# Attention products over 64 features with all 128 rows of TensorE in both passes

## The chip, the core and the metric

The kernel runs on one core of a Trainium2 chip: TensorE (the matrix engine, 128 rows by 128 columns), VectorE, ScalarE, GpSimd, the on-chip memory SBUF, the accumulators of TensorE in eight banks of PSUM, and DMA queues to HBM. The metric is the device time of one execution in microseconds, the median of several runs. TensorE's clock has two levels, 1.2 and 2.4 GHz; the profile gives the granted share of the higher one.

## What is computed

One encoder layer over 512 tokens of 1024 features: a SwiGLU FFN, a projection, sparse attention beside a gated convolution, an output projection, a second FFN and a gated embedding, each of the first parts with a layer norm. The attention chooses 128 keys for each query by an indexer and runs a softmax over these. All values are float32.

```python
x = layer_norm(A * x + 0.5 * swiglu(x, ffn1...))
q, k, v, qi, ki, wi, bg, cg, u = split(x @ w_in)      # 8 heads x 64; ki: 64; wi: 8
score = sum_h relu(qi[h] @ ki.T) * wi[h]              # chunk-causal keys only
idx = top_k(score, 128)
attn[h] = softmax(q[h] @ k[h][idx].T / 8 - slope[h] * |dist|) @ v[h][idx]
conv = bg * causal_conv3(cg * u)
x = layer_norm(A * x + concat(attn, conv) @ w_out)
x = layer_norm(A * x + 0.5 * swiglu(x, ffn2...))
out = x + sigmoid(x @ ple_gate_w) * (p @ ple_proj_w)
```

## The kernel before

Every float32 operand is split into a high part, rounded to the type that TensorE multiplies in one pass (`F32R`), and a low part, the rest. `split` (L110 to L112) does it: a ScalarE cast (L111), then a VectorE subtraction (L112). `mm` (L127 to L133) makes a product from three passes over such parts, high by high, high by low, low by high, one matmul each at L132, which is the line of nearly all matmuls.

Tokens are handled in four blocks of 128. The order of the work is: first FFN; the first block of values v; the indexer's keys `ki` and queries `qi`; the scores (L541 to L555: for query blocks 1 to 3, eight heads each, one product at L506 and L507, a ScalarE relu at L550, a VectorE accumulation at L552 or L554); the choice of keys (`choose`, L563 and L566, 16 rounds on VectorE) interleaved with TensorE's projections of v, the convolution and queries and keys (`qk_proj`), 24 matmuls each; attention; the output projection; the second FFN; the gate. A scheduler places the instructions of each engine in the order of the program, changed by priorities: weights are loaded and split ahead of their use by a number of instructions (`unit`, L114 to L122). Each engine then runs its own list in order.

A product over a head's 64 features does not use `mm`. `stack` (L492) puts the high parts of a head's queries on 64 of the 128 rows and the low parts on the other 64. `mm64` (L504 to L507) then takes two passes: both halves of the rows by the keys' high parts, which stand there twice (L506, 128 rows), and the high half alone by the keys' low parts (L507, 64 rows). The indexer's keys `ki` have high and low parts on both halves already. In `qk_proj` (L610) the high parts of a pair of heads' keys go to `kT[j]`, copied to the other half by ScalarE at L622; the low parts of two pairs share one page, `kL[j // 2]`, and stand on one half only. 24 such products belong to the scores, 32 to the logits.

In attention, `softmax(h)` (L665) makes four products of query block t by (t + 1) x 128 keys, and for each a VectorE pass from the bank (L676), an exponential on ScalarE (L677), a reciprocal and a multiplication on VectorE (L678, L679). `av(h)` (L681) transposes the ten 128 x 128 blocks of probabilities on TensorE (L693), splits them (three banks), pulls one item of filling work, and multiplies by v: for each of the four key blocks three passes of `mm` at L703 with the pair's 128 columns of v as weights, of which the head's 64 are used, into the one bank of the group "av". The split at L708 writes the head's half of `attnT[j]`. `softmax(h + 1)` is issued ahead of `av(h)`; two items of filling work (the last pair's projection, the convolution's rows of the output projection, the embedding's projection) come with each head. The pages of v hold all high parts, then all low parts.

Pages of 4 KiB a partition are taken from a list of 38, the one free for longest first.

Of the kernel before, what the change touches and what calls it, by code (L numbers as in the profile page):

```python
# [12 lines left out]
P = 128  # L13
# [15 lines left out]
# places on chip, and how far ahead of its use (in instructions) each kind of weights is asked for  # L29
# [34 lines left out]
def layer_kernel(ctx: ExitStack, tc: tile.TileContext, x, ln1_g, ln1_b, ffn1_wg, ffn1_wu, ffn1_wd, w_in,  # L64
# [17 lines left out]
    # 4 KiB pages, the one that has been free for longest first  # L82
# [31 lines left out]
    def unit(src, shape, ahead=AHEAD):  # L114
        """1024 weights a partition, loaded and split: pages of high and low parts."""
        with tc.high_priority(offset=ahead):
            r = page(shape, F32)
            nc.sync.dma_start(r, src)
            hi, lo = page(shape), page(shape)
            split(hi, lo, r)  # L120
            free(r)
        return hi, lo  # L122
# [4 lines left out]
    def mm(ps, pairs, first=True, last=True):  # L127
        """sum over pairs of (stationary (high, low), moving (high, low))"""
        n = len(pairs)
        for i, (st, mv) in enumerate(pairs):  # L130
            for k, (a, b) in enumerate(PASSES):
                nc.tensor.matmul(ps, lhsT=st[a], rhs=mv[b], start=first and i == 0 and k == 0,  # L132
                                 stop=last and i == n - 1 and k == 2)  # L133

    # ---- tokens on partitions (nat) and features on partitions (xT, high and low parts)
# [31 lines left out]
    def both(tile2, *idx):  # L167
        """(high, low) of a page [P, 2, n]"""
        return tuple(tile2[(slice(None), k) + idx] for k in range(2))

    # Operands of the seven products, by quarters: features' halves and tokens' halves
    class Quarters:
        """x, features on partitions: quarters (feature half, token half) and the sums of them"""
# [6 lines left out]
        def slot(self, name):  # L180
            """high and low parts' places"""
            if name in ("B11", "B21", "B22", "T1"):
                i = ("B11", "B21", "B22", "T1").index(name)
                self.q[name] = [self.big[k][:, i] for k in range(2)]
            else:
                self.q[name] = [page([P, 4, 256]) for k in range(2)]
                if name != "B12":
                    self.pages += self.q[name]
            return self.q[name]

        def block(self, t, group):
            """tokens' block t; returns the copies to be made of it"""
# [15 lines left out]
        def load(self, src, h, n):  # L208
            """a quarter from DRAM, features on rows there"""
            self.raw[h, n] = page([P, 4, 256], F32)  # L210
            nc.sync.dma_start(self.raw[h, n], rows(src[:, n * 256:(n + 1) * 256], h * 512, 4))
# [4 lines left out]
        def copies(self, todo):  # L216
            for r, p3, lo in todo:
                # one reader of a bank at a time
                cp = nc.scalar.copy(r, p3)
                tc.add_manual_dep(getattr(cp, "ins", cp), getattr(lo, "ins", lo).name,  # L220
                                  mybir.DependencyInfo(mybir.DependencyClass.Sync, mybir.DependencyReason.DATA), reason="bank")
# [17 lines left out]
    def ffn(X, wg, wu, wd, ln_g, ln_b, first, load_nat, groups, nplain, ahead, ahead_f, ahead_d):  # L239
        """nat <- LN(nat + 0.5 / alpha * swiglu(x)); returns its transpose."""  # L240
# [10 lines left out]
        def plain(fc, ws, cuts, ah):  # L251
            """one chunk of hidden features, each product computed"""
# [16 lines left out]
        def weights(w, fc, ops, pages):  # L269
            """the seven products' weights for two chunks, step by step: (high, low), [P, 4, P] each"""  # L270
# [31 lines left out]
        def two(fc, ah):  # L302
            """two chunks of hidden features by seven products"""
# [8 lines left out]
            def prod(a, b):  # L312
                """a product for gate and up"""
# [5 lines left out]
            # e: chunk by chunk, token halves of gate and up; k: partial sums  # L319
# [85 lines left out]
    # the per-layer embedding's input, features on partitions, and its weights  # L405
# [10 lines left out]
    def embed(t):  # L416
        """the per-layer embedding's projection"""
# [9 lines left out]
    # ---------------------------------------------------------------- start  # L427
# [3 lines left out]
    with tc.high_priority(offset=10000), tc.manual_schedule():  # L431
# [8 lines left out]
        # until x is there, the tensor engine warms up  # L440
# [18 lines left out]
    # ---------------------------------------------------------------- projections  # L459
    def colT(u, group, tok0=0, m=P):  # L460
        """columns' projection, features on partitions"""
        ps = bank(group)
        mm(ps[:m, :S - tok0], [((u[0][:, c], u[1][:, c]), (x1T[0][:, c, tok0:], x1T[1][:, c, tok0:])) for c in range(NDC)])
        free(*u)
        return ps[:, :S - tok0]
# [4 lines left out]
    # v, tokens on partitions  # L470
# [3 lines left out]
    def v_proj(blocks):  # L474
        for t in blocks:
            ps = bank("main")
            mm(ps, [((x1T[0][:, c, ts(t)], x1T[1][:, c, ts(t)]), (wv[c // 2][0][:, c % 2], wv[c // 2][1][:, c % 2])) for c in range(NDC)])
            v.append(page([P, 2, 512]))
            split(v[t][:, 0], v[t][:, 1], ps)
# [8 lines left out]
    # A product over a head's 64 features takes two passes: high and low parts of the queries, one above  # L488
    # the other, by the keys' high parts twice; then the queries' high parts by the keys' low parts.
    HALF = (slice(0, 64), slice(64, 128))  # L490

    def stack(dst, ps, scale=None):  # L492
        """two heads' queries: high parts where the head is, low parts in the other half"""
# [10 lines left out]
    def mm64(ps, q, e, at, k_hi, k_lo):  # L504
        """a head's queries by its keys"""
        nc.tensor.matmul(ps, lhsT=q[:, e, at], rhs=k_hi, start=True, stop=False)  # L506
        nc.tensor.matmul(ps, lhsT=q[HALF[e], e, at], rhs=k_lo[HALF[e]], start=False, stop=True)  # L507

    # indexer keys and weights, then queries
# [20 lines left out]
    # minus the distance, and minus BIG where a key isn't admissible or not among the chosen  # L530
# [10 lines left out]
    # scores and the choice of keys: query block 0 chooses every admissible key  # L541
# [33 lines left out]
    # short convolution  # L575
# [27 lines left out]
    # queries are scaled by 1 / (8 slope), exactly  # L603
# [6 lines left out]
    def qk_proj(j, group):  # L610
# [5 lines left out]
        kT[j] = page([P, 2, 512])  # L616
        if j % 2 == 0:
            kL[j // 2] = page([P, 2, 512])
        for e in range(2):
            here, there = HALF[e], HALF[1 - e]  # L620
            split(kT[j][here, e], kL[j // 2][here, j % 2], ps[here])
            nc.scalar.copy(kT[j][there, e], kT[j][here, e].bitcast(F32))  # L622
# [4 lines left out]
    def out_conv():  # L627
        """the convolution's rows of the output projection"""
# [32 lines left out]
    # attention, a head at a time  # L661
# [3 lines left out]
    def softmax(h):  # L665
        """exp(logits - max) / sum, queries on partitions"""
# [4 lines left out]
        for t in range(NTB):  # L671
# [3 lines left out]
            mm64(ps[:, :w_], qT[j], e, ts(t), kT[j][:, e, :w_], kL[j // 2][:, j % 2, :w_])  # L675
# [5 lines left out]
    def av(h, fill):  # L681
        j, e = h // 2, h % 2
        a = soft[h]
        # keys on partitions: blocks 0, then 1 and 3, then 2
# [17 lines left out]
        for b in range(NTB):  # L702
            mm(po[:, b * P:], [(both(v[b], slice(j * P, (j + 1) * P)), pT[b])], first=b == 0, last=b == NTB - 1)  # L703
# [3 lines left out]
        pr = slice(e * 64, (e + 1) * 64)  # L707
        split(attnT[j][pr, 0], attnT[j][pr, 1], po[pr])  # L708
# [5 lines left out]
    for h in range(NH):  # L714
# [4 lines left out]
        if h % 2:  # L719
            free(qT[h // 2], kT[h // 2])  # L720
        if h % 4 == 3:
            free(kL[h // 4])
# [3 lines left out]
    # output projection, attention's rows  # L726
# [23 lines left out]
    # ---------------------------------------------------------------- second FFN  # L750
    x3T = ffn(X, ffn2_wg, ffn2_wu, ffn2_wd, ln3_g, ln3_b, {}, None, GROUPS2, NPLAIN2, AHEAD2, AHEAD_F2, AHEAD_D2)

    # ---------------------------------------------------------------- per-layer embedding
# [41 lines left out]
```

## Time and profile before

| | us |
|---|---|
| median of 3 runs (1041.1 to 1044.16) | 1044.11 |
| span of the profiled execution | 1039.8 |
| TensorE matmuls busy | 1026.4 |
| VectorE busy | 819.2 |
| ScalarE busy | 432.7 |

The profiled execution is one run; its span goes from the first to the last instruction. A matmul's recorded duration holds its way through the array, so neighbours overlap; the distance between the starts of two matmuls tells what one takes of a full engine. Weight loads have rows of their own (PEld) and may lie under the matmul before. Line numbers are those of the kernel before.

### The profile page before, as it was taken

The numbers are of one execution on the slowest core, as the hardware profiler recorded it, in microseconds if no ns is written. First come the engines' busy times: TensorE is split into PE (matmuls) and PEld (weight loads), VectorE is DVE, ScalarE is ACT, GpSimd is POOL, SyncE is SP. The second block draws the span as 40 slices with busy tenths as digits, with TensorE's granted clock in tenths as the row PEclk, the third lists the DMA queues.
The fourth block names the chain that finished last, engine by engine and source line by source line (L and its number), as shares of the span: only waits on it lengthen the run. The fifth ranks groups of instructions, "written<-read, shape, count | busy, mean of one in ns | idle before, by whom it ended". The sixth has DMA issues, their size and how long they took to land.

```text
span 1039.8 us, 15540 instructions
## 1 busy us (share of the span) xinstructions
PE 1026.4 (99%) x6345; PEld 909.6 (87%) x6345; DVE 819.2 (79%) x1275; ACT 432.7 (42%) x605; POOL 24.9 (2%) x35
## 2 busy tenths in 40 slices
PE   8999999999999999999999999999999999999998
PEld 7989899898998785888877778989999899998887
DVE  7997868878798947999467889986877968688852
ACT  6444434334344335332565636442524434245221
POOL 1000000000001200000000001000000000000100
PEclk9999999999999999999999999999999999999999
DMA  9432324323236220422111323331424313227111
GB/s 315 134 119 82 105 79 143 101 82 122 82 132 184 61 81 21 132 72 74 48 61 61 102 61 102 99 103 44 162 82 140 103 59 105 83 83 255 50 49 51
DMA packets 99511, 104.59 MB, mean 101 GB/s; under 512 B 5872, under 2 KB 81904, under 8 KB 99440
## 3 DMA queue, kind: packets, MB, share of 16 engines
q1 hardware_dynamic: 99440, 103.60, 31.6%
q8 instruction: 50, 0.82, 0.3%
q14 instruction: 21, 0.17, 0.1%
HBM read 101.49 MB, written 2.10 MB: 100 GB/s over the span
## 4 chain that ended last, share of the span: by engine, by line
PE 93%; DMA 3%; DVE 2%; ACT 1%; issue 0%; POOL 0%; POOLq 0%; SPq 0%; DVEq 0%; ACTq 0%
PE bk L132 88%; PE bk L507 2%; PE bk L506 1%; ACT pg L111 1%; DMA pg<-in_w_in_dram 1%; PE bk L693 1%; DMA pg<-in_ffn_wu_dram 1%; DVE pg L112 1%; DMA pg<-in_x_t_dram 1%; DMA pg<-in_ffn_wd_dram 1%; PE bk L146 1%; DVE nat L162 0%; PE bk L201 0%; POOL mv L160 0%; DVE st L738 0%
## 5 line engine op out<-in xcount | busy, mean ns | idle before, releaser
L132 PE MATMUL bk<-pg,pg 128*128 128x256 f32 (+2 forms) x2928 | 512.3, 333 | 3.0 <-ACT pg L111 2.6
L132 PEld LDWEIGHTS bk<-pg,pg 128*128 128x128 f32 x2928 | 442.4, 190 | 58.5 <-ACT pg L111 4.7
L111 ACT CAST pg<-pg 128x1024 fp32r<-128x1024 f32 (+1 forms) x267 | 260.1, 985 | 312.5 <-PE bk L132 78.3
L112 DVE TENSOR_TENSOR pg<-pg,pg 128x1024 fp32r<-128x1024 f32 (+1 forms) x267 | 301.1, 1140 | 39.5 <-ACT pg L111 31.0
L132 PE MATMUL bk<-xq,pg 128*128 128x256 f32 x2208 | 274.2, 284 | 1.6 <-DVE pg L112 0.8
L132 PEld LDWEIGHTS bk<-xq,pg 128*128 128x128 f32 x2208 | 269.3, 192 | 4.5 <-ACT pg L111 1.8
L132 PE MATMUL bk<-xT,pg 128*128 128x512 f32 (+2 forms) x600 | 133.6, 382 | 0.3 <-ACT xT L111 0.2
L132 PEld LDWEIGHTS bk<-xT,pg 128*128 128x128 f32 (+1 forms) x600 | 109.8, 186 | 22.3 <-issue 0.6
L132 PE MATMUL bk<-pg,xT 128*128 128x512 f32 (+1 forms) x312 | 71.6, 381 | 1.4 <-DVE nat L385 1.4
L132 PEld LDWEIGHTS bk<-pg,xT 128*128 128x128 f32 x312 | 54.4, 188 | 14.6 <-issue 2.8
L329 ACT ACTIVATE a<-pg 128x512 f32<-128x512 f32 x40 | 25.2, 629 | 69.5 <-DVE pg L338 63.3
L111 ACT CAST pg<-hf 128x512 fp32r<-128x512 f32 x48 | 29.7, 618 | 37.0 <-DVE hf L330 19.7
L399 DVE SCALAR_TENSOR_TENSOR nat<-bk,nat 128x512 f32<-128x512 f32 x64 | 40.4, 684 | 0.8 <-PE bk L132 0.7
L112 DVE TENSOR_TENSOR pg<-bk,pg 128x512 fp32r<-128x512 f32 (+2 forms) x45 | 27.6, 637 | 14.5 <-ACT pg L111 14.2
L338 DVE TENSOR_TENSOR pg<-bk,pg 128x512 f32<-128x512 f32 x20 | 13.8, 692 | 31.7 <-PE bk L132 31.4
L111 ACT CAST pg<-bk 128x512 fp32r<-128x512 f32 (+2 forms) x45 | 23.0, 548 | 36.6 <-PE bk L132 33.4
L330 DVE TENSOR_TENSOR hf<-a,pg 128x512 f32<-128x512 f32 x40 | 27.6, 689 | 12.6 <-ACT a L329 12.6
L112 DVE TENSOR_TENSOR pg<-hf,pg 128x512 fp32r<-128x512 f32 x48 | 32.9, 686 | 4.2 <-ACT pg L111 4.2
L160 POOL TENSOR_TENSOR mv<-mv,mhalf 128x1 f32<-128x1 f32 x12 | 17.8, 1479 | 644.3 <-DVE mv L159 644.3
L286 DVE TENSOR_TENSOR pg<-pg,pg 128x512 f32<-128x512 f32 x40 | 27.3, 687 | 5.9 <-DMA pg<-in_ffn_wg_dram 5.9
L292 DVE TENSOR_TENSOR pg<-pg 128x512 f32<-128x512 f32 x40 | 27.5, 688 | 2.8 <-PE bk L132 2.8
L287 DVE TENSOR_TENSOR pg<-pg,pg 128x512 f32<-128x512 f32 x40 | 27.4, 687 | 0.0
(96 smaller groups left out, 589.7 us busy)
## 6 DMA issues: line engine op xcount, KB each, us to landing
pg<-in_ffn_wg_dram SPq DMA_DIRECT2D x44, 512.0 KB, 3.8
pg<-in_ffn_wu_dram SPq DMA_DIRECT2D x44, 512.0 KB, 4.7
pg<-in_ffn_wd_dram SPq DMA_DIRECT2D x44, 512.0 KB, 4.0
pg<-in_w_in_dram SPq DMA_DIRECT2D x28, 512.0 KB, 3.6
pg<-in_w_out_dram SPq DMA_DIRECT2D x8, 512.0 KB, 3.5
pg<-in_ple_gate_w_dram SPq DMA_DIRECT2D x8, 512.0 KB, 4.9
pg<-in_x_t_dram SPq DMA_DIRECT2D x4, 512.0 KB, 7.2
nat<-in_x_dram SPq DMA_DIRECT2D x4, 512.0 KB, 9.5
```

Source lines behind the costliest of these rows:

```text
L111: nc.scalar.copy(hi, src)
L112: nc.vector.tensor_sub(lo, src, hi.bitcast(F32))
L132: nc.tensor.matmul(ps, lhsT=st[a], rhs=mv[b], start=first and i == 0 and k == 0, stop=last and i == n - 1 and k == 2)
L160: nc.gpsimd.tensor_tensor(mv[:, 3:4], mv[:, 2:3], mhalf, op=ALU.pow)
L286: nc.vector.tensor_add(S1, A21, A22)
L287: nc.vector.tensor_sub(S2, S1, A11)
L292: nc.vector.tensor_sub(S3, A11, A21)
L329: nc.scalar.activation(s_t, e[m][:, :, 0], AF.Silu)
L330: nc.vector.tensor_mul(h3, s_t, e[m][:, :, 1])
L338: nc.vector.tensor_add(e[0][:, 1], prod("S4", "B22"), u4)
L399: nc.vector.scalar_tensor_tensor(dst, acc[t], CY, dst, op0=ALU.mult, op1=ALU.add)
L507: nc.tensor.matmul(ps, lhsT=q[HALF[e], e, at], rhs=k_lo[HALF[e]], start=False, stop=True)
```

## The change

The keys' low parts get a page of their own for each pair of heads and are copied to the other half of the rows as the high parts are, so that both passes of `mm64` use 128 rows, which adds the product of low by low parts. The values stand as 64 high and 64 low columns side by side for each head; one matmul then gives the high part's product on 64 rows of the output and the low part's on the other 64, for both parts of the probabilities: two passes instead of three. The two halves of the output are added: a ScalarE copy brings one half to the other's rows, and a VectorE addition writes the head's rows, from which the split is made. The rest of the diff removes comments.

```diff
 (v_proj)
-            v.append(page([P, 2, 512]))
-            split(v[t][:, 0], v[t][:, 1], ps)
+            v.append(page([P, NH, 2, HD]))
+            split(v[t][:, :, 0], v[t][:, :, 1], ps.rearrange("p (h d) -> p h d", h=NH))
 (mm64)
-        nc.tensor.matmul(ps, lhsT=q[HALF[e], e, at], rhs=k_lo[HALF[e]], start=False, stop=True)
+        nc.tensor.matmul(ps, lhsT=q[:, e, at], rhs=k_lo, start=False, stop=True)
 (qk_proj)
-        kT[j] = page([P, 2, 512])
-        if j % 2 == 0:
-            kL[j // 2] = page([P, 2, 512])
+        kT[j], kL[j] = page([P, 2, 512]), page([P, 2, 512])
         for e in range(2):
             here, there = HALF[e], HALF[1 - e]
-            split(kT[j][here, e], kL[j // 2][here, j % 2], ps[here])
-            nc.scalar.copy(kT[j][there, e], kT[j][here, e].bitcast(F32))
+            split(kT[j][here, e], kL[j][here, e], ps[here])
+            for z in (kT[j], kL[j]):
+                nc.scalar.copy(z[there, e], z[here, e].bitcast(F32))
 (softmax)
-            mm64(ps[:, :w_], qT[j], e, ts(t), kT[j][:, e, :w_], kL[j // 2][:, j % 2, :w_])
+            mm64(ps[:, :w_], qT[j], e, ts(t), kT[j][:, e, :w_], kL[j][:, e, :w_])
 (av)
-            mm(po[:, b * P:], [(both(v[b], slice(j * P, (j + 1) * P)), pT[b])], first=b == 0, last=b == NTB - 1)
+            vb = v[b][:, h].rearrange("p k d -> p (k d)")
+            for k in range(2):
+                nc.tensor.matmul(po[:, b * P:], lhsT=vb, rhs=pT[b][k], start=b == 0 and k == 0, stop=b == NTB - 1 and k == 1)
 ...
-        pr = slice(e * 64, (e + 1) * 64)
-        split(attnT[j][pr, 0], attnT[j][pr, 1], po[pr])
+        pr = HALF[e]
+        low, o = ring("hf", 2, [P, 512]), ring("hf", 2, [P, 512])
+        nc.scalar.copy(low[HALF[0]], po[HALF[1]])
+        nc.vector.tensor_add(o[pr], po[HALF[0]], low[HALF[0]])
+        split(attnT[j][pr, 0], attnT[j][pr, 1], o[pr])
 (after av of a pair's second head)
-            free(qT[h // 2], kT[h // 2])
-        if h % 4 == 3:
-            free(kL[h // 4])
+            free(qT[h // 2], kT[h // 2], kL[h // 2])
```

## Rows read from the trace of the kernel before

**Rows 1.** The page: busy time and share of the engines; clock by slices.
```profile
PE 1026.4 (99%) x6345; PEld 909.6 (87%) x6345; DVE 819.2 (79%) x1275; ACT 432.7 (42%) x605; POOL 24.9 (2%) x35
...
PEclk9999999999999999999999999999999999999999
```

**Rows 2.** The page: the chain that ended last, by line.
```profile
PE bk L132 88%; PE bk L507 2%; PE bk L506 1%; ACT pg L111 1%; DMA pg<-in_w_in_dram 1%; PE bk L693 1%; DMA pg<-in_ffn_wu_dram 1%; DVE pg L112 1%; DMA pg<-in_x_t_dram 1%; DMA pg<-in_ffn_wd_dram 1%; PE bk L146 1%; DVE nat L162 0%; PE bk L201 0%; POOL mv L160 0%; DVE st L738 0%
```

**Rows 3.** Stretches: length, busy PE, PEld, DVE, ACT, POOL, clock, DMA share, GB/s.
```profile
390.00:413.00 23.00, 23.00 (x77) 12.63 (x75) 15.50 (x37) 11.33 (x24) 0.00 (x0) 1.00 0.08 24
413.00:492.00 79.00, 79.00 (x344) 64.43 (x344) 76.76 (x180) 23.83 (x30) 0.00 (x0) 1.00 0.32 87
492.00:540.00 48.00, 48.00 (x210) 37.78 (x209) 25.05 (x54) 25.47 (x45) 0.00 (x0) 1.00 0.18 55
540.00:600.00 60.00, 59.98 (x287) 45.29 (x286) 47.46 (x132) 35.39 (x81) 0.00 (x0) 1.00 0.24 80
600.00:645.00 45.00, 44.43 (x246) 37.43 (x245) 38.51 (x61) 21.06 (x38) 5.82 (x4) 1.00 0.23 68
```

**Rows 4.** Timeline of TensorE, runs of L132: start, length, operation, shape, count.
```profile
530.56 8.46 PE L132 MATMUL bk<-xT,pg 128*128 128x512 f32 x36
538.86 1.25 PE L693 MATMUL bk<-ident,a 128*128 128x128 f32 x10
...
649.93 7.36 PE L132 MATMUL bk<-xq,pg 128*128 128x256 f32 x60
657.13 1.60 PE L132 MATMUL bk<-pg,pg 128*128 128x256 f32 x12
```

**Rows 5.** Timeline of TensorE, one head in attention.
```profile
550.15 1.25 PE L693 MATMUL bk<-ident,a 128*128 128x128 f32 x10
551.16 4.85 PE L132 MATMUL bk<-pg,pg 128*128 128x512 f32 x24
555.85 0.27 PE L506 MATMUL bk<-pg,pg 128*128 128x128 f32 x1
...
559.69 1.90 PE L132 MATMUL bk<-pg,pg 128*128 128x512 f32 x7
561.43 1.25 PE L693 MATMUL bk<-ident,a 128*128 128x128 f32 x10
```

**Rows 6.** Timeline of TensorE, score stage.
```profile
410.68 0.50 PE L132 MATMUL bk<-pg,xT 128*128 128x512 f32 x1
411.02 0.40 PE L506 MATMUL bk<-pg,pg 128*128 128x512 f32 x1
411.35 0.50 PE L507 MATMUL bk<-pg,pg 64*128 64x512 f32 x1
411.77 0.50 PE L132 MATMUL bk<-pg,xT 128*128 128x512 f32 x1
```

**Rows 7.** Line L507: loads (min, median, max ns), idle before, waits for it.
```profile
L507 PEld LDWEIGHTS bk<-pg,pg x56: 182/183/184, 390.3 to 598.0; 64*128 64x128 f32 x56
...
  issue: 12.2, 42
...
  DVE a L676: 12.7, 12
```

**Rows 8.** ScalarE by line, 522.5 to 600: count, busy us, mean ns, idle before.
```profile
L111 ACT CAST pg<-bk 64x512 fp32r<-64x512 f32 x10 | 5.8, 578 | 14.0 <-PE bk L132 13.9
...
L622 ACT CAST pg<-pg 64x512 fp32r<-64x512 f32 x4 | 2.5, 619 | 0.1
```

**Rows 9.** VectorE by line, 522.5 to 600.
```profile
L112 DVE TENSOR_TENSOR pg<-bk,pg 64x512 fp32r<-64x512 f32 x10 | 6.9, 688 | 0.3
```

**Rows 10.** Line L566, the choice of keys: durations, first and last start.
```profile
L566 DVE MATCH_REPLACE8 pg<-m,pg x48: 399/540/686, 401.9 to 485.8; 128x256 f32<-128x256 f32 x16, 128x384 f32<-128x384 f32 x16, 128x512 f32<-128x512 f32 x16
```

**Rows 11.** Timeline of TensorE, the first logits.
```profile
522.39 0.22 PE L506 MATMUL bk<-pg,pg 128*128 128x128 f32 x1
```

**Rows 12.** Waits of TensorE's weight loads, 520 to 660: total, times, longest.
```profile
PEld bk L132 <- ACT pg L111: 1.2, 4, 0.4
```

## What I predicted, and why

> **What bounds the kernel now.** I read the busy shares first. TensorE is busy 1026.4 us, 99% of the span, and the granted clock is in its top step in every slice; VectorE has 79%, ScalarE 42% [rows 1]. A busy share can hide pauses inside a matmul, so next comes the chain that ended last: 88% of it is the common product loop L132, only 3% the two lines L507 and L506 that the change touches [rows 2]. Third, the stretches from the index scores to the second FFN: TensorE is full in all of them up to 600 us; VectorE is nearly full while the keys are chosen (76.76 of 79 us), has room before and after, and less room in attention, 47.46 of 60 us [rows 3]. So what leaves TensorE's stream leaves the time, until VectorE fills up.
>
> **What one matmul should cost.** On a full engine the start-to-start distance counts, not the recorded duration. In long runs of L132 it is: 512 columns, from 530.56 to the next group at 538.86, 8.30 us for 36, of which the first still stands behind an L507, so 0.227 each; 256 columns, 649.93 to 657.13, 7.20 us for 60, 0.120 each [rows 4]. For 384 I take the middle, 0.173 (an estimate from these two), and for 128 the ten transposes between 550.15 and 551.16, 0.101 each [rows 5].
>
> **Part 1, the second pass of mm64 on 128 rows instead of 64.** The pass with 64 active rows is not cheap. In attention, from 555.85 to 561.43, stand four pairs of L506 and L507 (128, 256, 384 and 512 columns) with L132 between them, 1, 4 and 7 of 512 columns: 5.58 us against 2 x (0.101 + 0.120 + 0.173 + 0.227) + 12 x 0.227 = 3.97, so 0.40 us too much for each pair [rows 5]. In the score stage an L132, an L506 and an L507 of 512 columns start at 410.68, 411.02 and 411.35 and the next instruction at 411.77: 1.09 us for three matmuls that would take 3 x 0.227 = 0.68, an excess of 0.41 [rows 6]. Where it goes is seen at the weight loads: L507's own, 183 ns, has idle time ahead of it that nothing in the profile explains in 42 of 56 cases, 12.2 us in all [rows 7], and the L132 and L506 on either side are stretched from 0.227 to 0.34 and 0.33, so a load is not slipped under the matmul before it there. There are 56 pairs, 24 for scores (8 heads by 3 blocks) and 32 for logits (8 by 4). With 128 rows in both passes each load should go under the matmul before it as L132's do: 56 x 0.40 = 22.4 us off TensorE, 9.6 in the scores and 12.8 in attention. No row shows an L507 with 128 rows; the bounds are the L132 distance (gain 0.40) and no gain at all, and I take the L132 distance, since L506 differs from L132 in nothing but its neighbours.
>
> The Trainium skill speaks on both sides here. "TensorEngine Tiling (Array Packing)", Tiling Modes, Key Properties, says that a change of the tiling mode drains TensorE; the excess of 0.40 us around each L507 agrees. "TensorE: Matmul & The Clock Gate", in its table Why this matters for your kernels, says that a matmul over 32 rows takes the time of one over 128; by that, Part 1 would bring nothing and the sum would be Part 2's alone, the third rival below.
>
> **Part 2, two passes instead of three in av.** Each head issues 3 passes by 4 key blocks with 512, 384, 256 and 128 columns at L703, of which one pass goes: 0.227 + 0.173 + 0.120 + 0.101 = 0.62 us; 8 heads, 5.0 us, 32 matmuls. The remaining 64 keep 128 x 128 weights, so their price stays.
>
> **Part 3, the sum of a head's halves.** Each av adds a ScalarE copy of 64 x 512 out of the bank (0.58 us, the row of the 64 x 512 casts from a bank [rows 8]) and a VectorE addition of 64 x 512 (0.69 us, the subtraction of that size from a bank [rows 9]); the two split instructions stay, but read SBUF. ScalarE: 8 x 0.58 = 4.6 us, hidden, since it has 35.39 of 60 us busy [rows 3]. VectorE: 8 x 0.69 = 5.5 us, 7 of them before 600. The copy waits for av's last matmul as the cast did; queued behind it on ScalarE are the next softmax's exponentials. The addition waits for the copy, with the next head's L676 behind it on VectorE, and a second round trip (cast, subtraction) follows. The one "av" bank is free after copy and addition, as it was after cast and subtraction, so the next av doesn't wait longer for it. attnT comes 1.3 us later; only the output projection needs it, and of its first group nine matmuls on other heads' rows, 9 x 0.227 = 2.0 us, come ahead of the last pair's. If that cover fails it costs 1.3 us once.
>
> **Part 4, the key halves.** Each qk_proj adds two ScalarE copies of 64 x 512 at L622's price, 0.62 us [rows 8]: 8 x 0.62 = 5.0 us, in stretches where ScalarE is busy 23.83 of 79 and 25.47 of 48 us [rows 3]; the keys of the first heads are projected well before their logits. The low halves take four pages instead of two, freed with their pair: one or two fewer in a list that, counted along the program, holds 13 or more there, so some loads ask for a page that came free a turn later. That costs between 0 and a few us of one load's delay; 0, since TensorE waits for no load in attention now. No DMA is added or moved. The split of v writes runs of 64 elements: four times on each of two engines, between 0 and a doubling of 0.69, 2.8 us on VectorE; 0.
>
> **Where the gain meets VectorE.** In the scores VectorE has 15.50 of 23 us busy [rows 3]; the 21 pairs of that window give 21 x 0.40 = 8.4, which leaves 14.6, so VectorE would be 0.9 us late. What follows on it, the choice, has its last replacement at 485.8 [rows 10] while TensorE projects until the first logits at 522.39 [rows 11]: over 30 us of slack. The 9.6 us pass whole. From 492 to 540 VectorE has 25.05 of 48 us [rows 3]: the 8 pairs there, 3.2 us, pass. From 540 to 600 it is different: VectorE has 47.46 us and gets 7 x 0.69 = 4.8 more, 52.3. TensorE's 60 us lose 24 x 0.40 + 7 x 0.62 = 13.9 and would be 46.1. VectorE becomes the bound and lets 60 - 52.3 = 7.7 us through. After 600, head 7 brings 0.6 us. Sum: 9.6 + 3.2 + 7.7 + 0.6 = 21.1 us. The profiled execution has a span of 1039.8 us and the median of the runs is 1044.1, 4.3 us more around the span, which I keep: 1044.1 - 21.1 = 1023.0 us.
>
> **Rivals.** (a) TensorE stays the bound: VectorE's excess is carried into the 6.5 us that it has free after 600 [rows 3], since a softmax runs a head ahead of its transposes. Then 22.4 + 5.0 = 27.4 us go: 1016.7. Against it: 52.3 us of work in a stretch of 46. (b) VectorE doesn't run gapless, because each softmax and split goes to and fro between it and ScalarE: 540 to 600 gives nothing, 13.4 us in all, 1030.7. For it: even now VectorE stands 12.5 of 60 us there; against it: 12 of its waits, 12.7 us, are for L507 [rows 7], and shrink with it. (c) Rows don't matter, and the excess is a cost of changing operands that stays: only Part 2, 1044.1 - 5.0 = 1039.1. Against it: L132 changes operands too and shows no such pause. (d) Slower, through the end of a head: TensorE, in order, comes to the next head's transposes while ScalarE and VectorE hold the four steps, 0.58 + 0.69 + 0.62 + 0.69 = 2.58 us, in front of what it needs, plus 0.69 for VectorE's longer queue, in each head, and the key copies, 5.0 us, as well: 8 x 3.27 + 5.0 = 31.2 us against 27.4, 1047.9. It decides from a standstill of 27.4 / 8 = 3.4 us a head. Against it: all of TensorE's waiting for ScalarE's splits between 520 and 660 is 1.2 us, the longest 0.4 [rows 12].
>
> **How the numbers follow.** VectorE as the bound in attention, 1019 to 1027: 0.50. (a), below 1019: 0.20. (b), 1027 to 1036: 0.17. (c), about 1039: 0.05. Within 0.3% of before (1041 to 1047.2, about what a measurement of this kernel can tell from no change), a mixture of (b) and late loads: 0.05. (d): 0.03. Faster by over 0.3% so has 0.92, within 0.05, slower 0.03. The range reaches from (a) to (b) with 1.5 us on either side: 1015 to 1032.
>
> **What would show it.** Right: L507's distance at 512 columns falls from 0.42 to about 0.23 and no idle time stands ahead of its loads; av has 64 matmuls, not 96; the first logits start some 9 us earlier; in attention VectorE's busy share is above 95% and TensorE shows waits for VectorE or ScalarE. Wrong: an L507 that still holds 0.4 us (c), a gap-free TensorE in attention (a), or a TensorE that stands at each head's end (d).

## The result: 1026.2 us, and where the time went

The changed kernel takes 1026.18 us (median of 4 runs, 1026.09 to 1031.11), the kernel before 1042.61 us in the same comparison; the ratio is 0.9855 with an interval of 0.9828 to 0.9882, that is 15 us or 1.5% faster (16.4 us between the two medians). The profiled executions have spans of 1039.8 and 1024.0 us.

The page of the changed kernel, busy times, clock and the chain that ended last:

```profile
PE 1004.6 (98%) x6313; PEld 903.8 (88%) x6313; DVE 822.2 (80%) x1283; ACT 441.8 (43%) x621; POOL 25.0 (2%) x35
...
PE 89%; DMA 4%; DVE 3%; ACT 3%; issue 1%; POOLq 0%; SPq 0%; ACTq 0%
PE bk L132 86%; ACT pg L111 2%; DVE pg L112 1%; DMA pg<-in_ffn_wu_dram 1%; PE bk L506 1%; DMA pg<-in_w_in_dram 1%; DMA pg<-in_x_t_dram 1%; PE bk L507 1%; PE bk L704 1%; DMA pg<-in_ple_proj_w_dram 1%; DMA pg<-in_ffn_wd_dram 0%; PE bk L146 0%; ACT a L676 0%; DMA pg<-in_ple_gate_w_dram 0%; PE bk L692 0%
```

Against [rows 1, 2]: TensorE is busy 21.8 us less and has 32 matmuls less, but the span falls by 15.8 only, and ScalarE and VectorE have 3% of the chain each (1% and 2% before). (From here, L704 is the values' product, L692 the transposes, L675 to L678 the softmax, L710 and L711 the new copy and addition, L739 the output projection's addition.)

Line L507 in the changed kernel, as in [rows 7]:

```profile
L507 PEld LDWEIGHTS bk<-pg,pg x56: 187/189/192, 391.6 to 581.2; 128*128 128x128 f32 x56
...
its engine sat idle before it (us, times) until:
who waited for it (us, times):
  DVE a L675: 1.7, 3
```

No load has idle time ahead of it now; before it was 12.2 us in 42 places. VectorE's waits for L507 went from 12.7 to 1.7 us. The timeline of TensorE in the score stage, as in [rows 6]:

```profile
405.79 0.40 PE L132 MATMUL bk<-pg,xT 128*128 128x512 f32 x1
406.02 0.39 PE L506 MATMUL bk<-pg,pg 128*128 128x512 f32 x1
406.25 0.40 PE L507 MATMUL bk<-pg,pg 128*128 128x512 f32 x1
406.49 1.08 PE L132 MATMUL bk<-pg,xT 128*128 128x512 f32 x4
```

L132, L506 and L507 now start 0.23, 0.23 and 0.24 us apart, 0.70 us where it was 1.09. The same view in attention, one head, as in [rows 5]:

```profile
549.29 1.25 PE L692 MATMUL bk<-ident,a 128*128 128x128 f32 x10
550.30 3.00 PE L132 MATMUL bk<-pg,pg 128*128 128x512 f32 x12
553.13 1.37 PE L704 MATMUL bk<-pg,pg 128*128 128x512 f32 x8
...
554.86 1.55 PE L132 MATMUL bk<-pg,pg 128*128 128x512 f32 x6
557.06 0.45 PE L506 MATMUL bk<-pg,pg 128*128 128x384 f32 x1 [0.64 <-DVE ss L675]
...
559.35 0.92 PE L692 MATMUL bk<-ident,a 128*128 128x128 f32 x7
```

A head takes 10.06 us from transposes to transposes instead of 11.28, and for the first time TensorE stops in it: at 557.06 it waits for VectorE to have read a logits' bank.

**TensorE's account.** To see where the rest stayed I price every matmul at the distances of the forecast (0.227, 0.173, 0.120 us; 0.104 for 128 columns) and take the sum from the start-to-start distances. What is left are stops; time that a lower clock costs is counted among them. The priced work is 993.2 us before and 988.2 in the changed kernel. The stops, in us:

| stretch | before | changed | e2 | e4 | e5 | e7 | e9 | e11 | e12 |
|---|---|---|---|---|---|---|---|---|---|
| start to first score | 11.8 | 13.3 | 13.0 | 11.8 | 14.1 | 11.3 | 11.7 | 12.1 | 11.8 |
| scores to first logits | 9.6 | 1.5 | 9.5 | 1.4 | 1.4 | 1.4 | 1.5 | 1.4 | 1.4 |
| first logits to head 0's transposes | 3.1 | 0.6 | 3.1 | 0.6 | 0.6 | 0.6 | 0.7 | 0.6 | 0.2 |
| head 0's to head 7's transposes | 10.5 | 7.0 | 10.5 | 5.0 | 6.0 | 6.0 | 5.1 | 6.9 | 4.2 |
| to the last block's transposes | 1.8 | 5.0 | 6.5 | 2.3 | 2.4 | 4.0 | 5.6 | 1.3 | 3.1 |
| second FFN | 2.4 | 1.2 | 1.2 | 1.1 | 1.2 | 1.6 | 2.7 | 2.9 | 3.9 |
| gate | 1.8 | 1.6 | 3.4 | 2.6 | 1.5 | 2.9 | 3.4 | 1.6 | 1.4 |

Of the stops before, 22.0 us stood around the 56 L507; all of these are gone. With 5.0 us of work that makes 27.0. New stops take 11.2 us back: 15.8 remain, the difference of the spans. The rest is on what these new stops are.

### The profile page after: what moved, and what is told of

The parts are those of the page before. It is cut to its first block, busy times and chain, and to the rows that moved or that the text cites. A ratio compares the mean times of both kernels' runs of the same rounds, so it can differ in the third digit from the quotient of the medians.

```text
span 1024.0 us, 15507 instructions
## 1 busy us (share of the span) xinstructions
PE 1004.6 (98%) x6313; PEld 903.8 (88%) x6313; DVE 822.2 (80%) x1283; ACT 441.8 (43%) x621; POOL 25.0 (2%) x35
## 4 chain that ended last, share of the span: by engine, by line
PE 89%; DMA 4%; DVE 3%; ACT 3%; issue 1%; POOLq 0%; SPq 0%; ACTq 0%
PE bk L132 86%; ACT pg L111 2%; DVE pg L112 1%; DMA pg<-in_ffn_wu_dram 1%; PE bk L506 1%; DMA pg<-in_w_in_dram 1%; DMA pg<-in_x_t_dram 1%; PE bk L507 1%; PE bk L704 1%; DMA pg<-in_ple_proj_w_dram 1%; DMA pg<-in_ffn_wd_dram 0%; PE bk L146 0%; ACT a L676 0%; DMA pg<-in_ple_gate_w_dram 0%; PE bk L692 0%
## 5 line engine op out<-in xcount | busy, mean ns | idle before, releaser
L132 PE MATMUL bk<-pg,pg 128*128 128x256 f32 (+1 forms) x2832 | 496.4, 333 | 4.4 <-ACT pg L111 1.8
L132 PEld LDWEIGHTS bk<-pg,pg 128*128 128x128 f32 x2832 | 427.6, 190 | 56.0 <-ACT pg L111 2.6
L132 PE MATMUL bk<-xq,pg 128*128 128x256 f32 x2208 | 275.3, 284 | 4.6 <-DVE mv L158 1.5
L132 PEld LDWEIGHTS bk<-xq,pg 128*128 128x128 f32 x2208 | 270.6, 193 | 7.0 <-ACT pg L111 2.3
L132 PE MATMUL bk<-xT,pg 128*128 128x512 f32 (+2 forms) x600 | 133.0, 381 | 0.3 <-ACT xT L111 0.2
L132 PEld LDWEIGHTS bk<-xT,pg 128*128 128x128 f32 (+1 forms) x600 | 109.9, 186 | 21.5 <-ACT xT L111 0.5
L132 PE MATMUL bk<-pg,xT 128*128 128x512 f32 (+1 forms) x312 | 69.5, 374 | 1.3 <-DVE nat L385 1.3
L132 PEld LDWEIGHTS bk<-pg,xT 128*128 128x128 f32 x312 | 55.0, 188 | 11.4 <-ACT pg L111 1.8
L111 ACT CAST pg<-hf 128x512 fp32r<-128x512 f32 (+1 forms) x56 | 34.6, 618 | 35.2 <-DVE hf L330 19.6
L112 DVE TENSOR_TENSOR pg<-hf,pg 128x512 fp32r<-128x512 f32 (+1 forms) x56 | 38.3, 684 | 4.7 <-ACT pg L111 4.5
L286 DVE TENSOR_TENSOR pg<-pg,pg 128x512 f32<-128x512 f32 x40 | 27.3, 686 | 5.7 <-DMA pg<-in_ffn_wg_dram 5.7
L112 DVE TENSOR_TENSOR pg<-bk,pg 128x512 fp32r<-128x512 f32 (+2 forms) x37 | 22.5, 626 | 8.5 <-ACT pg L111 8.1
L287 DVE TENSOR_TENSOR pg<-pg,pg 128x512 f32<-128x512 f32 x40 | 27.3, 685 | 0.0
L293 DVE TENSOR_TENSOR pg<-pg,pg 128x512 f32<-128x512 f32 x40 | 27.1, 686 | 0.1
```

The lines of the kernel that those rows point to most:

```text
L111: nc.scalar.copy(hi, src)
L112: nc.vector.tensor_sub(lo, src, hi.bitcast(F32))
L286: nc.vector.tensor_add(S1, A21, A22)
L287: nc.vector.tensor_sub(S2, S1, A11)
L293: nc.vector.tensor_sub(S4, A12, S2)
```

## The experiments

The kernel before took between 1042.1 and 1043.0 us in the comparisons below; each ratio is against it.

**e1: the scores alone.** The kernel before, 128 rows in the indexer's second pass only.

```diff
-            mm64(ps[:, :w_], qi[h // 2], h % 2, ts(t - 1), ki[:, 0, :w_], ki[:, 1, :w_])
+            nc.tensor.matmul(ps[:, :w_], lhsT=qi[h // 2][:, h % 2, ts(t - 1)], rhs=ki[:, 0, :w_], start=True, stop=False)
+            nc.tensor.matmul(ps[:, :w_], lhsT=qi[h // 2][:, h % 2, ts(t - 1)], rhs=ki[:, 1, :w_], start=False, stop=True)
```

> The kernel before with one edit: the second pass of the 24 score products takes all 128 rows; the logits keep 64 rows, the values three passes. No copy, addition or page is added. If the 64 rows cost TensorE 0.40 us a pair, the scores give 24 x 0.40 = 9.6 us, or the 8.1 us that the changed kernel shows between its first score and its first logit: 1033 to 1034.5 us against 1042.6. If the gain of the whole change came from elsewhere (the fewer passes, a shifted order), this kernel stays at 1042 to 1043.

Measured: 1034.79 us, ratio 0.992 (0.9906 to 0.9934): 8.3 us by the ratio (7.4 between the medians) from one operand's rows in 24 instructions, with nothing else touched. Its trace has 8.1 us less of stops between the first score and the first logits, as the changed kernel's. About half of the whole gain is this.

**e2: the values alone.** The kernel before with the new v, the two passes, copy and addition, and L507 as it was.

```diff
-            mm(po[:, b * P:], [(both(v[b], slice(j * P, (j + 1) * P)), pT[b])], first=b == 0, last=b == NTB - 1)
+            vb = v[b][:, h].rearrange("p k d -> p (k d)")
+            for k in range(2):
+                nc.tensor.matmul(po[:, b * P:], lhsT=vb, rhs=pT[b][k], start=b == 0 and k == 0, stop=b == NTB - 1 and k == 1)
...
+        nc.scalar.copy(low[HALF[0]], po[HALF[1]])
+        nc.vector.tensor_add(o[pr], po[HALF[0]], low[HALF[0]])
```

> The kernel before with the two passes over the values alone (values stored by heads, copy and addition of the halves); scores and logits keep their 64-row pass. TensorE loses 32 matmuls, 5.0 us, and is still the slowest engine in attention with its 32 slow pairs (about 55.6 us of matmuls from 540 to 600 against 52.3 us on VectorE). If that is what bounds, 1037.6 us. If the added round trip between ScalarE and VectorE at a head's end holds TensorE up, the gain is gone or turned: 1042 or more.

Measured: 1042.38 us, ratio 1.0002 (0.999 to 1.0014). The 32 matmuls are gone and TensorE's stops within the heads are as before (10.5 us), but the time does not move. From the first head's transposes to the last's it takes 63.7 us instead of 66.6; behind them that is lost again. The stops between the last head's transposes and the last block's rise from 1.8 to 6.5 us. The waits of TensorE's matmuls there (603 to 645 us):

```profile
PE bk L132 <- DVE nat L742: 3.5, 2, 3.1
```

L742 is there what L739 is in the changed kernel: an output projection's product waits 3.1 us for a bank that VectorE has yet to read. In the stretch from 632 to 636 of this execution the granted clock averages 0.62, so a part of the 6.5 us is the clock after that wait.

**e3: both passes on 64 rows.** The queries' low parts by the keys' high parts are left out.

```diff
-        nc.tensor.matmul(ps, lhsT=q[:, e, at], rhs=k_hi, start=True, stop=False)
+        nc.tensor.matmul(ps, lhsT=q[HALF[e], e, at], rhs=k_hi[HALF[e]], start=True, stop=False)
```

> The kernel before with 64 rows in the first pass of mm64 too, so that the queries' low parts by the keys' high parts are left out of scores and logits. If the cost lies in the change between 128 and 64 rows, an L506 followed by its L507 holds 0.23 us at 512 columns as in a long run, instead of 0.33, and the cost stays only where an L132 stands beside the pair (0.43 behind the pair's end or start). If it lies in 64 rows as such, both lines hold about 0.43 us at 512 columns wherever they stand.

Measured: 1035.4 us in one run. The timeline of TensorE, first the neighbouring pairs at the start of the scores, then one between products of 128 rows:

```profile
391.02 0.28 PE L506 MATMUL bk<-pg,pg 64*128 64x256 f32 x1
391.15 0.27 PE L507 MATMUL bk<-pg,pg 64*128 64x256 f32 x1
391.26 0.28 PE L506 MATMUL bk<-pg,pg 64*128 64x256 f32 x1
...
405.95 0.50 PE L132 MATMUL bk<-pg,xT 128*128 128x512 f32 x1
406.38 0.50 PE L506 MATMUL bk<-pg,pg 64*128 64x512 f32 x1
406.72 0.39 PE L507 MATMUL bk<-pg,pg 64*128 64x512 f32 x1
407.04 0.96 PE L132 MATMUL bk<-pg,xT 128*128 128x512 f32 x3
```

Among themselves matmuls of 64 rows start 0.11 to 0.13 us apart at 256 columns, as those of 128 rows do (0.120). Between products of 128 rows the three still take 1.09 us, spread over all three (0.43, 0.34 and 0.32; for L506 the expectation had 0.23). So 64 rows as such cost nothing; going from one row count to the other and back costs 0.4 us, 0.2 for each change on average. The two pages that the forecast weighed do not exclude each other. The Trainium skill says in "TensorE: Matmul & The Clock Gate", Why this matters for your kernels, that a matmul over 32 rows takes the time of one over 128; the run of 64-row matmuls agrees with it. The Trainium skill says in "TensorEngine Tiling (Array Packing)", Tiling Modes, Key Properties, that a change of the tiling mode drains TensorE; the 0.4 us there and back agree with it, though no run shows what TensorE does in that time. The kernel before paid for the change of rows; the one run of e3 is faster too, with a product left out.

**e4: the changed kernel without the sum.** The product with the values' low parts is left out.

```diff
-        low, o = ring("hf", 2, [P, 512]), ring("hf", 2, [P, 512])
-        nc.scalar.copy(low[HALF[0]], po[HALF[1]])
-        nc.vector.tensor_add(o[pr], po[HALF[0]], low[HALF[0]])
-        split(attnT[j][pr, 0], attnT[j][pr, 1], o[pr])
+        split(attnT[j][pr, 0], attnT[j][pr, 1], po[HALF[0]])
```

> The changed kernel without the ScalarE copy and the VectorE addition of the halves: the product with the values' low parts is left out, and the split reads the bank. VectorE loses 8 x 0.69 = 5.5 us and ScalarE 8 x 0.58 = 4.6 us in attention; TensorE's instructions are the same. If VectorE bounds attention there, the stops of 6.3 us that TensorE has gained between the first logits and the last head's transposes shrink by 4 to 5 us: about 1021 to 1022 us against 1026.2. If the stops come from something else (the order of the queues, loads, banks), it stays within 1 us of 1026.

Measured: 1022.0 us, ratio 0.9799 (0.9785 to 0.9814), 4 to 6 us better than the changed kernel. This spoke for VectorE as the bound, but the stops within the heads fall only from 7.0 to 5.0 us; those behind them fall from 5.0 to 2.3. Copy, addition and two hand-overs went together here, so it doesn't say which of them counts.

**e5: scores and logits alone.** The changed kernel's `mm64` and `qk_proj`, with the three passes of before over the values.

```diff
-            for k in range(2):
-                nc.tensor.matmul(po[:, b * P:], lhsT=vb, rhs=pT[b][k], start=b == 0 and k == 0, stop=b == NTB - 1 and k == 1)
+            mm(po[:, b * P:], [(both(v[b], slice(j * P, (j + 1) * P)), pT[b])], first=b == 0, last=b == NTB - 1)
```

> The kernel before with 128 rows in both passes of scores and logits and the keys' low parts on both halves; the values keep their three passes, and there is no copy and addition of halves. TensorE loses 56 x 0.39 = 22 us, VectorE gets nothing more (47.5 us of the stretch of 60, of which TensorE needs 60 - 9.6 = 50.4). If VectorE is what took the gain back in the changed kernel, TensorE is the bound again and nearly all 22 us come: 1020 to 1022 us, faster than the changed kernel's 1026.2. If TensorE stops anyway once its products are quick (the order of the queues, the round trips with ScalarE), about 6 us are lost as there: 1026 to 1028. If the values' two passes carry a part of the gain, it is slower than the changed kernel: 1031.

Measured: 1028.15 us (1025.71 to 1030.16), ratio 0.9856 (0.9837 to 0.9875), the changed kernel's own ratio. The first theory's 1020 to 1022 is missed. VectorE is less loaded here, and TensorE stops nearly as much within the heads (6.0 against 7.0 us). The stretch from the first head's transposes to the last's in the kernel before, the changed kernel, e5 and e7, the views of each (columns as in [rows 3]):

```profile
538.86:605.42 66.56, 66.54 (x327) 50.96 (x326) 53.43 (x142) 39.95 (x91) 0.00 (x0) 1.00 0.22 72
```

```profile
529.77:589.38 59.61, 56.70 (x302) 46.27 (x301) 53.81 (x146) 44.85 (x100) 0.00 (x0) 1.00 0.26 89
```

```profile
530.55:593.93 63.38, 61.25 (x333) 51.16 (x332) 53.08 (x142) 41.88 (x94) 0.00 (x0) 1.00 0.25 84
```

```profile
527.81:585.79 57.98, 55.98 (x298) 45.72 (x297) 47.58 (x122) 45.19 (x100) 26.58 (x25) 1.00 0.27 92
```

VectorE is busy for 80% before, 90% in the changed kernel, 84% in e5 and 82% in e7. TensorE's stops (1.2 beside those around L507 before, then 7.0, 6.0 and 6.0) do not follow that share.

**e6: no sum for the last head.** Its product with the values' low parts is left out.

```diff
+        if h < NH - 1:
             nc.scalar.copy(low[HALF[0]], po[HALF[1]])
             nc.vector.tensor_add(o[pr], po[HALF[0]], low[HALF[0]])
             split(attnT[j][pr, 0], attnT[j][pr, 1], o[pr])
+        else:
+            split(attnT[j][pr, 0], attnT[j][pr, 1], po[HALF[0]])
```

> The changed kernel without copy and addition for the last of the eight heads alone, whose product with the values' low parts is left out. VectorE loses one 0.69 us. If the longer chain of the last head is what makes TensorE stop 3 us more around the output projection than before, the kernel gains 2 to 3 us: about 1023.5. If that stop comes from VectorE's work of all heads, or from the order in which weights are split there, it gains under 1 us: 1025.5 to 1026.2.

Measured: 1024.91 us, ratio 0.9827 (0.9813 to 0.9841). The profiled span is 1.3 us shorter than the changed kernel's, and 1.2 of that lies ahead of the first score, where the two programs are the same; the stops behind the last head are 4.6 us against 5.0. The longer chain of the last head is not what holds TensorE there.

**e7: the division on GpSimd.**

```diff
-            nc.vector.tensor_scalar(a[:, o], a[:, o], st[:, t, 2:3], None, op0=ALU.mult)
+            nc.gpsimd.tensor_scalar(a[:, o], a[:, o], st[:, t, 2:3], None, op0=ALU.mult)
```

> The changed kernel with the multiplication by the softmax's reciprocal (the 32 instructions of L678, 1.5 us a head on VectorE, 12 us in all) on GpSimd instead of VectorE. If VectorE's amount of work bounds attention, TensorE's stops there shrink from 8 us to about 2: 1020 to 1022 us. If GpSimd slows VectorE's own instructions or its results come too late for the transposes, the time stays at 1026 or rises.

Measured: 1023.45 us, ratio 0.9812 (0.9798 to 0.9825). All 32 multiplications left VectorE, whose share in attention fell to 82%, and the stops within the heads went from 7.0 to 6.0 us. The forecast for VectorE's amount of work was about 2. GpSimd's slower results are not what keeps them up: TensorE's weight loads wait for them once, 0.8 us, and for the logits' banks still 4.4 us. So the amount of VectorE's work is not by itself what sets the stops. What VectorE itself waits for in the changed kernel, between the first and the last head's transposes:

```profile
DVE pg L112 <- ACT pg L111: 3.5, 6, 1.7
DVE ss L677 <- ACT a L676: 1.5, 2, 1.2
DVE hf L711 <- ACT hf L710: 0.6, 1, 0.6
```

These 5.6 us of waiting for ScalarE and its 53.8 us of work fill the 59.6 us; it waits for TensorE 0.2 us, where it was 12.1 us before. With less to do it waits longer for ScalarE: 7.8 us in e7, 8.4 in e5.

**e8: the sum on GpSimd** for seven heads.

```diff
+            nc.scalar.copy(o[HALF[0]], po[HALF[0]])
+            nc.gpsimd.tensor_tensor(o[pr], o[HALF[0]], low[HALF[0]], op=ALU.add)
+            nc.scalar.copy(attnT[j][pr, 0], o[pr])
+            nc.gpsimd.tensor_tensor(attnT[j][pr, 1], o[pr], attnT[j][pr, 0].bitcast(F32), op=ALU.subtract)
```

> The changed kernel with the sum of the halves and the low part's subtraction of seven heads on GpSimd (2 x 0.69 us a head less on VectorE, 9.7 us in all) and one more ScalarE copy of 64 x 512 a head (0.58 us); the last head as in the changed kernel. If VectorE's amount of work bounds attention, most of the gain of the kernel without the sum comes without leaving anything out: 1021 to 1023 us. If ScalarE's longer queue or GpSimd's use of the memory takes its place, 1025 or more.

Measured: 1024.67 us, ratio 0.9826 (0.9811 to 0.9842): between the two expectations. The stops within the heads are 6.9 us, as in the changed kernel, although 9.7 us left VectorE. ScalarE got one copy more a head and TensorE's order changed with it, so this run alone would not decide.

**e9: five banks in one ring.** This asks for the wait itself instead of the load.

```diff
-BANKS = ((0, 1), (4, 5), (6,), (7, 2, 3))
+BANKS = ((0, 1), (4, 5, 7, 2, 3), (6,), ())
...
-            ps = bank("pt")
+            ps = bank("qk")
```

> The changed kernel with one ring of five banks for the logits and the transposed probabilities instead of two and three. If TensorE's stops at L506 come from its two banks (an L506 waits until VectorE has read the bank two products earlier), the 2.2 us that these stops take in attention fall below 0.5 and the time to about 1024 against 1026.2, or, both without a stretch at half clock, 1022.5 against 1024.6. If VectorE as a whole is late, the stop moves to the transposes or the values' products and the time stays within 1 us.

Measured: 1025.64 us, ratio 0.9838 (0.9823 to 0.9854). The waits of TensorE's weight loads in attention, the changed kernel (515 to 590 us) and e9 (514 to 584 us):

```profile
PEld bk L506 <- DVE ss L675: 3.5, 6, 1.1
PEld bk L704 <- ACT pg L111: 2.0, 4, 0.6
PEld bk L132 <- DVE pg L112: 1.3, 1, 1.3
PEld bk L704 <- DVE pg L112: 0.8, 3, 0.3
```

```profile
PEld bk L704 <- ACT pg L111: 3.2, 4, 1.3
PEld bk L704 <- DVE pg L112: 1.3, 4, 0.5
...
PEld bk L506 <- DVE ss L675: 0.4, 2, 0.2
```

The logits' wait for their two banks is gone (3.5 to 0.4 us), and a part of it comes back as a wait of the values' products for the split of the transposed probabilities (2.8 to 4.5 us). Within the heads 1.9 us are gained, 7.0 to 5.1. Behind them 0.6 are lost, in the second FFN 1.5 and in the gate 1.8, so the span is no shorter.

**e10: the weights 250 instructions ahead** (`AHEAD2 = 250` in the changed kernel).

> The changed kernel with the second FFN's first weights asked for, and split, 250 instructions ahead instead of 400. In the changed kernel VectorE splits two such units just ahead of the output projection's additions at L739, and TensorE stops 2.0 us there for a bank and 1.7 us at the first products of the second FFN. If the place of these splits is the cause, the stops from the last head's transposes to the last block's fall from 5 us to about 2: 1023 us against 1026.2. If VectorE's work of the layer norms alone bounds that stretch, it stays; if the weights then come too late, the second FFN starts later and the time rises by the length of a load and a split, 3 us or more.

Measured: 1026.74 us, ratio 0.9855 (0.9832 to 0.9879). Every engine's order came out as in the changed kernel, so it tells nothing on the question; it is a second measurement of the changed kernel, with the same ratio. Its trace repeats each row of the table within 0.5 us but the first, which is 1.1 us lower: differences of that size in the table say nothing.

**e11: the weights when they are due** (`AHEAD2 = 0`). In the changed kernel VectorE's order around the output projection's first block is this (timeline):

```profile
598.25 0.69 DVE L739 SCALAR_TENSOR_TENSOR nat<-bk,nat 128x512 f32<-128x512 f32 x1 [0.63 <-PE bk L132]
599.17 1.23 DVE L112 TENSOR_TENSOR pg<-pg,pg 128x1024 fp32r<-128x1024 f32 x1 [0.23 <-ACT pg L111]
...
601.12 1.23 DVE L112 TENSOR_TENSOR pg<-pg,pg 128x1024 fp32r<-128x1024 f32 x1 [0.72 <-ACT pg L111]
602.26 0.69 DVE L740 BATCH_NORM_STATS2 st<-nat 128x6 f32<-128x512 f32 x1
602.87 1.27 DVE L739 SCALAR_TENSOR_TENSOR nat<-bk,nat 128x512 f32<-128x512 f32 x2
603.60 1.19 PE L132 MATMUL bk<-pg,pg 128*128 128x512 f32 x4 [0.84 <-DVE nat L739]
```

Two splits of the second FFN's weights stand between the first and the second addition, wait for ScalarE, and TensorE waits for the bank behind them. In the kernel before, the second addition (L737 there) came ahead of the second split:

```profile
613.43 1.23 DVE L112 TENSOR_TENSOR pg<-pg,pg 128x1024 fp32r<-128x1024 f32 x1 [0.43 <-ACT pg L111]
614.58 0.68 DVE L737 SCALAR_TENSOR_TENSOR nat<-bk,nat 128x512 f32<-128x512 f32 x1
615.55 1.23 DVE L112 TENSOR_TENSOR pg<-pg,pg 128x1024 fp32r<-128x1024 f32 x1 [0.29 <-ACT pg L111]
```

> The changed kernel with the second FFN's first weights split when they are due, AHEAD2 = 0 (the edit to 250 left the order of every engine as it was, so that kernel was the changed kernel once more). Here VectorE's two splits of 1.23 us no longer stand ahead of the output projection's additions. If their place is what makes TensorE stop there, the excess between the last head's transposes and the last block's falls from 5 us to 2 or 3: about 1023 to 1024 us against 1026.2. If the second FFN then waits for its weights, what is gained is lost behind it, and the time stays or rises by 1 to 4 us. If the layer norms' own work bounds the stretch, the excess there stays at 5 us.

Measured: 1023.85 us, ratio 0.9827 (0.9803 to 0.9852). The timeline of e11 at the same place:

```profile
593.39 10.80 PE L132 MATMUL bk<-pg,pg 128*128 128x512 f32 x46
596.93 1.29 DVE L739 SCALAR_TENSOR_TENSOR nat<-bk,nat 128x512 f32<-128x512 f32 x2 [0.61 <-PE bk L132]
```

With the splits out of the way TensorE runs 46 products on end, and the stops of this stretch fall from 5.0 to 1.3 us, below the kernel before. The second FFN gives 1.7 us of it back. The intervals of the two ratios overlap, so the gain is read from the traces: from the first score to the end 630.4 us, against 632.5 in the changed kernel and 632.9 in e10.

**e12: the three together**, five banks, division on GpSimd and `AHEAD2 = 0`.

> The changed kernel with three edits together: one ring of five banks for logits and transposed probabilities, the multiplication by the reciprocal on GpSimd, and AHEAD2 = 0. If the places where TensorE stops are separate, their gains add up: about 2 us in attention from the banks, 1 us from the multiplication and 2 us from the output projection's stretch, some 5 us in all, so 1021 us against 1026.2, or 1019.6 against 1024.6 where no stretch at half clock falls in. If one stop only takes another's place (the values' products wait for ScalarE, the second FFN for its weights), it stays at the 1023.5 of the multiplication alone or above.

Measured: 1023.75 us, ratio 0.9825 (0.9807 to 0.9842). The stops within the heads are the lowest of all, 4.2 us, but the weight loads of the transposes now wait 2.0 us for GpSimd near the end of attention, and the second FFN's stops are the highest, 3.9. Within the heads the gains of the banks and of the multiplication add up (7.0 - 1.9 - 1.0 = 4.1); behind them most of that is lost. Of the kernels that compute everything e7 has the lowest ratio, 0.9812, but its interval overlaps those of e11 and e12, and from the first score to the end its trace takes 632.3 us, e12's 630.0.

## Why the prediction was right, step by step, and where it was not

The forecast was 1023.0 us with a range of 1015 to 1032; measured 1026.2.

**Part 1 was right**, in cause and size. 56 x 0.40 = 22.4 us were expected on TensorE; 22.0 stood around L507 and are gone. e1 shows one of its two pieces, the scores, in the time, e3 that the change of rows is the cause and not the rows.

**Part 2 was right as a count and wrong as a gain.** 5.0 us of work left TensorE. In the time no gain of it can be told: none alone (e2, 1.0002), and the kernel without it is as fast as with it (e5 against the changed kernel, 0.9856 and 0.9855). From the first score to the end the two traces differ by 1.4 us, not by 5.0. The step that failed is the last one of Part 3, that the added chain is hidden or costs 1.3 us once, and "After 600, head 7 brings 0.6 us". There the stops rose by 3.2 us.

**"The 9.6 us pass whole"** was nearly so: the stops from the first score to the first logits fell by 8.1 us. The other 1.5 are new stops at L506 and L507; their weight loads wait 2.5 us for ScalarE's relu, which reads the scores' banks. The first logits start 6.6 us earlier, not "some 9".

**"VectorE becomes the bound and lets 7.7 us through"** has the right size by luck. From head 0's to head 7's transposes the time fell by 66.56 - 59.61 = 6.95 us, where 12.7 were to be had: 9.3 of the pairs' stops and 3.4 of priced work. What came back are new stops, which rose from 1.2 to 7.0 us there. The 7.7 were worked out from 4.8 us more work on VectorE; its busy time in this stretch rose by 0.4 only (53.43 to 53.81): six additions came, but two splits (1.2 and 0.4 us) are placed elsewhere, and in a full queue instructions recorded with 0.69 us start 0.61 apart (602.26 and 602.87 in the timeline of the changed kernel under e11), so that the recorded lengths count too much. VectorE is at 90%, not above 95%, and taking 10 to 12 us of work off it (e7, e8) removes 1.0 and 0.1 us of stops. What fills its time up are 5.6 us of waiting for ScalarE, and what TensorE waits for are single results: a bank of the logits, the split of a transposed block. That is rival (b)'s mechanism, the going to and fro between VectorE and ScalarE, with less than half of its price: (b) let nothing through, and here 5.8 of the 12.7 us came back. e9 shows TensorE's wait directly for the banks. Whether the order of ScalarE's or VectorE's queue sets what remains, these runs don't settle.

**After the heads** e11 shows what the stops hang on: two splits of weights that VectorE does ahead of the second addition. The scheduler made a new order for the changed kernel, and in the order of the kernel before only one split stood there. The other traces fit in the main: e2 has both splits there and 6.5 us of stops; e4 and e5 have two additions ahead of the first split and 2.3 and 2.4 us. e6, with one split there, still stops 4.6 us, so the place of the splits is not all of it. Why the sum's presence brings this order about was not traced.

**The base.** The forecast kept 4.3 us around the span. It is 1026.09 - 1024.0 = 2.1 in the changed kernel's profiled run, and 1042.2 us in e1's comparison for the kernel before goes with a span of 1040.2, so 2.0. The other 2.2 were the difference between two executions. This error hid a part of the miss: with 2.1 the forecast would have been 1020.8, 5.3 us below the profiled 1026.1 and not 3. From the span alone the forecast gain of 21.1 stands against 15.8: it was a third too high. It splits into 1.4 at the start (below), 1.5 in the scores, 0.8 from the first logits to the first transposes, 0.7 in the heads and 3.4 behind them (2.8 lost where 0.6 were counted); from the second FFN on 2.7 came back.

## What to carry to other kernels

On a full TensorE, look at start-to-start distances around the odd shape: a product on half the rows among full ones cost 0.4 us however small it was, and filling the rows, here with copies that add a term of no need, was cheaper than leaving them out. When a change speeds up the bounding engine by a few per cent, count its own saving as an upper bound: here 4 parts in 10 came back, most of them as waits for single results, in an order of the queues that the change itself had altered. Test a suspected bound by moving work off the suspect before believing it, and look at what it waits for: VectorE at 90% looked full of work, and with less work it waited longer for ScalarE.

## What the runs showed of the hardware

- **The change of rows**: 0.2 us of TensorE's time on average for each change between 64 and 128 rows, none within a run of either (e3, at 256 columns).
- **GpSimd's pace**: in e7 its multiplications of 128 x 512 take three times VectorE's (481 ns in the kernel before):

```profile
L678 POOL TENSOR_SCALAR a<-a,ss 128x512 f32<-128x512 f32 x8 | 12.8, 1606 | 1.7 <-DVE ss L677 1.7
```

  and its additions of 64 x 512 in e8 take 1.40 us against 0.68.
- **The clock at the start.** In the profiled run of the changed kernel the granted clock is at its lower level for a part of the stretch from 8 to 16 us (0.89 from 8 to 12, 0.68 from 12 to 16); in that of the kernel before it is not, with the same instructions up to there. The stretch from 12 to 16 us of the kernel before, then of the changed kernel:

```profile
12.00:16.00 4.00, 4.00 (x34) 3.83 (x33) 4.00 (x5) 3.51 (x4) 0.00 (x0) 1.00 1.19 299
```

```profile
12.00:16.00 4.00, 4.00 (x26) 4.00 (x26) 4.00 (x4) 3.51 (x4) 0.00 (x0) 0.68 1.19 301
```

  TensorE does 26 matmuls there instead of 34. The first score comes 1.4 us later (391.56 against 390.13); 0.5 of that stands already at 11.04 us, where TensorE had waited for VectorE (0.88 us, 0.58 before). The first row of the table, the same program in all kernels, reaches from 11.3 to 14.1 us. The clock is not all of the spread between executions: of the 51 of the kernel before that the experiments are compared with, 12 at a mean clock of 1.000 have a median of 1041.6 us and 27 at 0.998 one of 1042.7, but these 27 alone reach from 1041.2 to 1044.9.
